# Opening stage of a two-layer hybrid trunk: own buffers for two streams of loads, and a written order on TensorE

## The chip, the core and the metric

The kernel runs on one core of a Trainium2 chip. The time is device microseconds of one execution, from several executions of the same program. The engines are named as the profile names them: PE (TensorE, products), PEld (its weight loads), DVE (VectorE), ACT (ScalarE), POOL (GpSimd) and SP (SyncE, whose queue issues the weight loads). Each engine works through its own instructions in the order in which they were built; semaphores tie the engines together.

## The reference, cut to what matters

Two layers run over 128 context tokens and 128 latent tokens that share all weights; the kernel takes both as one block of 256 columns. Ahead of each layer stand modulation vectors (shift, scale, gate) from a product of a conditioning vector with `w_mod`, and a normalisation that uses them:

```
m = jax.nn.silu(cond) @ w_mod + b_mod          # 2048 -> 6 x 2048, for c_ctx and for c
h = _rms_norm(x, norm1_g) * (1.0 + scale1) + shift1
p = h @ w_in                                   # gq gk gv gr glr aq ak av dqkv dz da db
```

Then follow gated linear attention, softmax attention and a gated DeltaNet on the parts of `p`, an output product, and a squared-ReLU MLP of four times the width. The opening stage of the kernel is the first layer's `m` (shift1 and scale1 only), `h`, and that part of `p` which needs only the first half of the 2048 inputs.

## The kernel before, in words

All products are made in three parts: a weight tile `raw` of 128 x 1024 numbers is loaded by SP (line 212, or 620 for the narrower first projection tiles), ACT copies it to `hi` in a shorter format, DVE makes `lo`, the rest, and PE multiplies `hi` with both halves of the activations and `lo` with the first. `hi` and `lo` have three buffers each.

`first_phase` (line 562) is the opening. It first makes `rstd`, the norm of each token. Then it walks over 16 chunks of 128 inputs, here called columns, n = 0 to 15:

- four modulation slices are loaded (line 593) and multiplied with the conditioning vectors (line 595, tile `mod0`, shown as mod); each slice makes 4 products, which the profile counts as 8 passes;
- ACT copies the result to `msb`; two small products turn it (line 601, `mod0t`); DVE adds the bias (`modc`), makes the scale `s` and the scaled chunk `ht`; ACT and DVE make both halves of the chunk `act` (`h_chunk`, line 492);
- for n < 8, two projection tiles are loaded, split and multiplied with the chunk (lines 619 to 633): 14 units of 3 products, into seven banks `fb`, `fbm`, `fbn`. At n = 7 the banks are copied out;
- for n >= 8, instead, a share of 45 half jobs is done (line 611): 3 tiles of `w_in` and 12 of `w_tok`, 3 steps each, which read only chunks 0 to 7 (tiles `g` and `gt`).

`mod0` and `mod0t` share one bank in `pmod`, so a column's slices can be multiplied only when DVE has read the turned result of the column before. All loads of the stage take buffers of one ring, `raw0`, with six buffers. A second ring of six, `wraw`, serves everything behind the opening.

The program is not issued in the order in which it is written: a scheduler with its own estimates orders each engine's instructions. Only products that bear the same token (`tok`, line 630: those of lines 631 to 633) keep their written order among each other. So the scheduler was free to set slices, turns and half jobs among the blocks, and to issue loads of the next stage early. The token of a product is given in `mm` (line 85).

Of the kernel before, what the change touches and what calls it, by code (L numbers as in the profile page):

```python
# [10 lines left out]
F32 = mybir.dt.float32  # L11
# [3 lines left out]
AF = mybir.ActivationFunctionType  # L15
ALU = mybir.AluOpType
AX = mybir.AxisListType
P = 128
# [23 lines left out]
def tile_hybrid_step(ctx: ExitStack, tc: tile.TileContext, A: dict, O: dict):  # L42
# [17 lines left out]
    ve, se = Timed(nc.vector, 1 / 960, 0.13), Timed(nc.scalar, 1 / 1400, 0.27)  # L60

    def pool(name, bufs=1, **kw):
        return tc.tile_pool(name=name, bufs=bufs, **kw)
# [3 lines left out]
    wraw = ctx.enter_context(pool("wraw", 6))  # L67
# [8 lines left out]
    pmod = ctx.enter_context(pool("pmod", 1, space=PS))  # L76
    dram = ctx.enter_context(pool("dram", 2, space=bass.MemoryType.DRAM))

    ntok = [0]

    def newtok():
        ntok[0] += 1
        return f"tok{ntok[0]}"

    def mm(out, lhsT, rhs, start=True, stop=True, tok=None, **kw):
        i = nc.tensor.matmul(out, lhsT=lhsT, rhs=rhs, start=start, stop=stop, **kw)  # L86
        n = math.prod(rhs.shape[1:])
        pe_t[0] += max(n / 2400 * (1 if rhs.dtype == F32R else 4), 0.027)
        if tok is not None:
            tc.stamp_issue_order_token(i.ins, tok)  # L90
        return i
# [39 lines left out]
    def open_act(tag, side="left"):  # L131
        st = ExitStack()
        pl = st.enter_context(pool(tag, side=side))
        return pl.tile([P, 16, 516], F32R, tag="act", name="act"), st

    act, actctx = open_act("acta")
# [19 lines left out]
    raw0 = rawctx.enter_context(pool("raw0", NRAW))  # L156
# [58 lines left out]
    def split_half(src, pl=None):  # L215
        raw = load_half(src, pl)
        hi = whi.tile([P, 1024], F32R, tag="hi", name="hi")
        lo = wlo.tile([P, 1024], F32R, tag="lo", name="lo")
        se.activation(hi, raw, AF.Copy)
        ve.tensor_tensor(lo, raw, hi.bitcast(F32), ALU.subtract)  # L220
        return hi, lo
# [66 lines left out]
    def gemm_pieces(src, halves, rhs_of, evac, pl=None):  # L288
        ps = pg.tile([P, 256], F32, tag="g", name="g")
        k0, k1 = 8 * halves[0], 8 * halves[-1] + 7  # L290
        for half in halves:
            hi, lo = split_half(src(half), pl)
            for q in range(2):
                for kk in range(4 * q, 4 * q + 4):
                    k = half * 8 + kk
                    a = rhs_of(k)
                    h = hi[:, kk * P : kk * P + P]
                    mm(ps, h, a[:, 0:256], start=(k == k0), stop=False)
                    mm(ps, h, a[:, 256:512], start=False, stop=False)
                yield  # L300
            for kk in range(8):
                k = half * 8 + kk
                mm(ps, lo[:, kk * P : kk * P + P], rhs_of(k)[:, 0:256], start=False, stop=(k == k1))
            if half == halves[-1]:
                evac(ps)
            yield
            if tick():
                yield
# [234 lines left out]
    def tsrc(w, n):  # L543
        return lambda half: w[n, half]

    def part_of(j):
        if j < 8:
            return lay["dqk"][:, j, :].rearrange("p (g t) -> p g t", g=2)
        if j < 12:
            return lay["vt"][:, :, (j - 8) * P : (j - 7) * P]  # L550
        t = lay["misc"] if j == 12 else lay["gqk"][:, j - 13, :]
        return t.rearrange("p (g t) -> p g t", g=2)

    def gq3(ps):
        return ps.rearrange("p (g t) -> p g t", g=2)

    def tok_dest(u, g):
        if u == 0:
            return lay["gv"][:, g, :]
        return lay["aq"][:, g, (u - 1) * 512 : u * 512] if u < 3 else lay["akv"][:, g, :]  # L560

    def first_phase(raw0):
        modc, s12, bm, ng = mods[0]
        X["np"] = raw0
        for n in range(16):
            accum_sq(n, n == 0)
        rate[0] = 0
        rstd = get_rstd()
        nb = len(FIRST)
        banks = [pg.tile([P, 512], F32, tag="g", name="fb") for _ in range(2)]  # L570
        banks += [pm.tile([P, 512], F32, tag="m", name="fbm") for _ in range(3)]
        banks += [pn.tile([P, 512], F32, tag="m", name="fbn") for _ in range(2)]
        tok = newtok()

        def half_jobs():
            for j in HALF_D:
                def evac(ps, j=j):
                    se.activation(part_of(j), gq3(ps), AF.Copy)

                yield from gemm_pieces(tsrc(A["w_in"][0], j), (0,), lambda k: act[:, k, 0:512], evac, raw0)  # L580
            for u in HALF_T:
                yield from gemm_tok(
                    lambda q, u=u: A["w_tok"][0][u, q], range(4),
                    lambda ps, g, u=u: se.activation(tok_dest(u, g), ps, AF.Copy), raw0,
                )

        jobs = half_jobs()
        njobs = 3 * len(HALF_D) + 12 * len(HALF_T)
        done = 0
        for n in range(16):  # L590
            ps = pmod.tile([P, 512], F32, tag="mod", name="mod0")
            for q in range(4):
                raw = load_half(A["w_mod0"][n, q], raw0)
                for kk in range(4):
                    mm(ps[32 * kk : 32 * kk + 32, 0:256], sc[:, 2 * (4 * q + kk) : 2 * (4 * q + kk) + 32], raw[:, kk * 256 : kk * 256 + 256],
                       start=(q == 0), stop=(q == 3), tile_position=(0, 32 * kk))
            msb = nrm.tile([P, 512], F32, tag="msb", name="msb")
            se.activation(msb[:, 0:256], ps[:, 0:256], AF.Copy)
            pt = pmod.tile([P, 512], F32, tag="mod", name="mod0t")
            for m in range(2):  # L600
                mm(pt[:, 2 * m : 2 * m + 2], msb[:, m * P : m * P + P], sel2)
            ve.tensor_tensor(
                modc[:, 0:2, n, :], pt[:, 0:4].rearrange("p (m c) -> p m c", m=2), bc(bm[:, 0:2, n], 2), ALU.add
            )
            ve.tensor_scalar(s12[:, 0, n, :], modc[:, 1, n, :], 1.0, ng[:, 0, n : n + 1], ALU.add, ALU.mult)
            t = X["np"].tile([P, 256], F32, tag="ht", name="ht", bufs=2)
            for g in range(2):
                s = slice(g * P, g * P + P)
                ve.scalar_tensor_tensor(t[:, s], X["x"][:, n, s], s12[:, 0, n, g : g + 1], rstd[:, s], ALU.mult, ALU.mult)
            h_chunk(n, t, modc[:, 0])  # L610
            if n >= 8:
                want = (n - 7) * njobs // 8
                while done < want:
                    next(jobs, None)
                    done += 1
                continue
            w = nb * 64
            for part in range(2):
                raw = raw0.tile([P, 1024], F32, tag="raw", name="raw")
                nc.sync.dma_start(raw[:, 0:w], A["w_in0"][n, part])  # L620
                hi = whi.tile([P, 1024], F32R, tag="hi", name="hi")
                lo = wlo.tile([P, 1024], F32R, tag="lo", name="lo")
                se.activation(hi[:, 0:w], raw[:, 0:w], AF.Copy)
                ve.tensor_tensor(lo[:, 0:w], raw[:, 0:w], hi[:, 0:w].bitcast(F32), ALU.subtract)
                for j in range(nb // 2):
                    u = part * (nb // 2) + j
                    o = banks[u // 2][:, (u % 2) * 256 : (u % 2) * 256 + 256]
                    h = hi[:, j * P : j * P + P]
                    l_ = lo[:, j * P : j * P + P]
                    kw = dict(tok=tok, skip_group_check=True)  # L630
                    mm(o, h, act[:, n, 0:256], start=(n == 0 and u % 2 == 0), stop=False, **kw)
                    mm(o, h, act[:, n, 256:512], start=False, stop=False, **kw)
                    mm(o, l_, act[:, n, 0:256], start=False, stop=(n == 7), **kw)
            if n == 7:
                for u, j in enumerate(FIRST):
                    src = gq3(banks[u // 2][:, (u % 2) * 256 : (u % 2) * 256 + 256])
                    if u % 4 < 2:
                        se.activation(part_of(j), src, AF.Copy)
                    else:
                        ve.tensor_copy(part_of(j), src)  # L640
        for _ in jobs:
            pass

# [9 lines left out]
    for l in range(L):  # L653
# [6 lines left out]
        else:  # L660
# [6 lines left out]
            act, actctx = nact, nactctx  # L667
# [157 lines left out]
        else:  # L825
            nlead = list(zip(FIRST, first))
            for j in FIRST[len(first) : 13]:
                for _ in range(2):
                    if nlead:
                        u, ps = nlead.pop(0)  # L830
# [841 lines left out]
```

## Time and profile before

| | |
|---|---|
| median of 3 runs | 2547.51 us (2547.04 to 2550.62) |
| the profiled execution | 2549.01 us, of which the span is 2547.2 us |
| mean granted clock | 0.993 |
| PE busy | 2482.5 us, 97% of the span |
| DVE, ACT busy | 1836.3 us (72%), 1246.1 us (49%) |

The span is what the profiler saw from the first instruction to the last; the time of the execution has some 2 us around it. Matmul ends in the profile are modelled, so that rows of PE can overlap a little: the distance between two starts tells more than a length. A number of passes (x8, x32) counts each product of 32-bit numbers twice. A wait in square brackets is the idle time of that engine just ahead of the row, with what ended it.

### The profile page before, as it was taken

Reading aid. Unit: us, or ns where it says so; the run is one execution under the profiler, and the core shown is the slowest. Engines: PE = TensorE matmul, PEld = TensorE weight load, DVE = VectorE, ACT = ScalarE, POOL = GpSimd, SP = SyncE. Lnnn points to the kernel's source line nnn. Section 1 sums busy time; section 2 is a strip of 40 time slices with the busy share of each in tenths; the row PEclk is TensorE's granted clock in tenths of the full one; section 3 lists DMA queues with packets and bytes.
Section 4 is the critical chain, followed back from the end, with each engine's and each line's share of the span. In section 5 each row is a group of like instructions: output and inputs, shape, how many; then the busy total and the mean of one; then the engine's idle time right before and its main releaser. Section 6 shows DMA issues by size and latency. Waiting matters only on the chain.

```text
span 2547.2 us, 47725 instructions
## 1 busy us (share of the span) xinstructions
PE 2482.5 (97%) x18796; PEld 2240.5 (88%) x18796; DVE 1836.3 (72%) x3478; ACT 1246.1 (49%) x2073; POOL 72.3 (3%) x108
## 2 busy tenths in 40 slices
PE   6999999999999999999999999999999999999999
PEld 4777677789899999999999888889999989999888
DVE  3456767658988898898897676786796564564665
ACT  3356244447554454444455763455675445445433
POOL 1000000000000100100100000000000000000000
PEclk9999999999999999999999999999999999999999
DMA  9975767785899999989996743446576666566564
GB/s 361 325 264 185 269 213 277 278 305 174 301 337 347 356 332 330 351 320 347 354 322 234 252 147 117 148 125 213 175 258 218 184 190 190 183 190 188 186 197 141
DMA packets 178993, 629.36 MB, mean 247 GB/s; under 512 B 21280, under 2 KB 28000, under 8 KB 177616
## 3 DMA queue, kind: packets, MB, share of 16 engines
q1 hardware_dynamic: 165600, 600.12, 68.4%
q0 software_dynamic: 10768, 22.94, 3.4%
q8 instruction: 148, 2.42, 0.4%
q10 hardware_dynamic: 2400, 3.24, 0.4%
q14 instruction: 77, 0.63, 0.1%
HBM read 613.62 MB, written 6.31 MB: 243 GB/s over the span
## 4 chain that ended last, share of the span: by engine, by line
PE 52%; ACT 1%; DVE 0%; DMA 0%; issue 0%; DVEq 0%; ACTq 0%
PE g L86 42%; PE gt L86 3%; PE gl L86 3%; PE mod L86 1%; PE ga L86 0%; ACT hi L56 0%; PE eb L86 0%; PE scb L86 0%; PE oatb L86 0%; PE xt L86 0%; PE yb L86 0%; PE ob L86 0%; PE bcb L86 0%; DMA x<-spill 0%; PE obg L86 0%; ACT L56 0%
## 5 line engine op out<-in xcount | busy, mean ns | idle before, releaser
L56 ACT ACTIVATE hi<-raw 128x1024 fp32r<-128x1024 f32 (+1 forms) x742 | 781.0, 1057 | 928.8 <-PE g L86 625.9
L56 DVE TENSOR_TENSOR lo<-raw,hi 128x1024 fp32r<-128x1024 f32 (+1 forms) x742 | 903.4, 1220 | 406.0 <-ACT hi L56 387.5
L86 PE MATMUL g<-act,hi 128*128 128x256 f32 (+1 forms) x7488 | 1053.5, 291 | 11.9 <-DVE x L56 3.8
L86 PEld LDWEIGHTS g<-act,hi 128*128 128x128 f32 x7488 | 955.6, 189 | 82.1 <-issue 22.3
L86 PE MATMUL g<-act,lo 128*128 128x256 f32 x4000 | 558.0, 282 | 2.8 <-DVE lo L56 2.8
L86 PEld LDWEIGHTS g<-act,lo 128*128 128x128 f32 x4000 | 512.8, 189 | 15.7 <-issue 4.8
L86 PE MATMUL g<-hid,hi 128*128 128x256 f32 (+1 forms) x1536 | 261.0, 319 | 0.0
L86 PEld LDWEIGHTS g<-hid,hi 128*128 128x128 f32 x1536 | 217.2, 189 | 22.1 <-ACT hi L56 4.2
L56 DVE SCALAR_TENSOR_TENSOR x<-g,modc,x 128x128 f32<-128x128 f32 x352 | 113.1, 348 | 149.5 <-PE g L86 144.3
L56 DVE CUSTOM_DVE_ANT_0 junk<-mraw,sb,bm 128x1024 bf16<-128x1024 f32 x160 | 205.0, 1281 | 2.4 <-DMA sb<-scd 0.9
L86 PE MATMUL mod<-raw,sc 128*32 128x512 f32 (+1 forms) x1216 | 144.1, 530 | 26.3 <-DMA raw<-w_mod 24.4
L56 DVE CUSTOM_DVE_ANT_0 junk<-mraw,sb,part 128x1024 bf16<-128x1024 f32 x128 | 164.1, 1282 | 5.2 <-DMA sb<-scd 4.7
L86 PE MATMUL gt<-hi,act 128*128 128x512 f32 x512 | 143.6, 412 | 3.9 <-ACT hi L56 3.9
L86 PE MATMUL g<-hid,lo 128*128 128x256 f32 x1024 | 141.6, 281 | 0.0
L86 PEld LDWEIGHTS g<-hid,lo 128*128 128x128 f32 x1024 | 134.5, 189 | 6.3 <-DVE x L56 0.8
L86 PEld LDWEIGHTS gt<-hi,act 128*128 128x128 f32 x512 | 94.8, 192 | 39.7 <-issue 11.1
L86 PEld LDWEIGHTS mod<-raw,sc 128*32 128x32 f32 x1216 | 29.4, 110 | 60.8 <-DMA raw<-w_mod 16.4
L86 PE MATMUL gt<-lo,act 128*128 128x512 f32 x256 | 75.1, 401 | 0.0
L86 PE MATMUL gl<-hid,hi 128*128 128x258 f32 x384 | 70.3, 286 | 2.1 <-ACT hi L56 2.1
L56 ACT ACTIVATE ffr<-g 128x256 f32<-128x256 f32 x116 | 42.9, 370 | 55.1 <-PE g L86 55.1
L56 ACT ACTIVATE xd<-g,modc 128x128 f32<-128x128 f32 x96 | 29.7, 360 | 68.1 <-PE g L86 68.1
L86 PEld LDWEIGHTS gl<-hid,hi 128*128 128x128 f32 x384 | 59.3, 189 | 2.6 <-ACT hi L56 2.5
(355 smaller groups left out, 1980.4 us busy)
## 6 DMA issues: line engine op xcount, KB each, us to landing
raw<-w_ff SPq DMA_DIRECT2D x512, 512.0 KB, 4.5
raw<-w_mod SPq DMA_DIRECT2D x240, 512.0 KB, 6.0
mraw<-w_modT SPq DMA_DIRECT2D x144, 512.0 KB, 6.2
raw<-w_in SPq DMA_DIRECT2D x86, 512.0 KB, 4.4
raw<-w_tok SPq DMA_DIRECT2D x64, 512.0 KB, 4.4
raw<-w_out SPq DMA_DIRECT2D x64, 512.0 KB, 4.3
sb<-scd POOLq DMA_DIRECT2D x9, 1024.0 KB, 9.5
raw<-w_in SPq DMA_DIRECT2D x16, 448.0 KB, 5.9
```

What stands on the lines that cost most here:

```text
L56: return f(out, *a, **kw)
L86: i = nc.tensor.matmul(out, lhsT=lhsT, rhs=rhs, start=start, stop=stop, **kw)
```

## The change

The opening's loads are put on two rings: the projection tiles of lines 619 and the half jobs go to `wraw`, the modulation slices keep `raw0`. The loop is written in another order, and while it runs every product of the stage bears one token, so PE keeps the written order: slices of column n + 1, then the block (or the half jobs) of column n, then the turn of column n + 1 and its chunk.

```diff
         i = nc.tensor.matmul(out, lhsT=lhsT, rhs=rhs, start=start, stop=stop, **kw)
...
+        if tok is None:
+            tok = cur[0]
         if tok is not None:
             tc.stamp_issue_order_token(i.ins, tok)
...
-                yield from gemm_pieces(tsrc(A["w_in"][0], j), (0,), lambda k: act[:, k, 0:512], evac, raw0)
+                yield from gemm_pieces(tsrc(A["w_in"][0], j), (0,), lambda k: act[:, k, 0:512], evac)
...
-                    lambda ps, g, u=u: se.activation(tok_dest(u, g), ps, AF.Copy), raw0,
+                    lambda ps, g, u=u: se.activation(tok_dest(u, g), ps, AF.Copy),
...
-        for n in range(16):
+
+        def columns(n):
             ps = pmod.tile([P, 512], F32, tag="mod", name="mod0")
...
+            return msb
+
+        def chunk(n, msb):
             pt = pmod.tile([P, 512], F32, tag="mod", name="mod0t")
...
+
+        def outer(n):
             w = nb * 64
             for part in range(2):
-                raw = raw0.tile([P, 1024], F32, tag="raw", name="raw")
+                raw = wraw.tile([P, 1024], F32, tag="raw", name="raw")
...
+        cur[0] = newtok()
+        chunk(0, columns(0))
+        for n in range(16):
+            msb = columns(n + 1) if n < 15 else None
+            if n < 8:
+                outer(n)
+            else:
+                want = (n - 7) * njobs // 8
+                while done < want:
+                    next(jobs, None)
+                    done += 1
+            if n < 15:
+                chunk(n + 1, msb)
+        cur[0] = None
```

How the order of the instructions moves is shown at three places. First PE, around the end of a block in the middle of the opening, before (x4 here is one slice, the numbers behind mod name the column):

```order
L86 MATMUL fbn<-act,hi 128x256 x2
L86 MATMUL fbn<-act,lo 128x256
L86 MATMUL mod_718<-raw,sc 32x256 x4
L86 MATMUL mod0t<-c_sel_97,msb 128x2 x2
L86 MATMUL mod_811<-raw,sc 32x256 x12
L86 MATMUL fb<-act,hi 128x256 x2
```

and the same place after:

```order
L86 MATMUL fbn<-act,hi 128x256 x2
L86 MATMUL fbn<-act,lo 128x256
L86 MATMUL mod0t<-c_sel_97,msb 128x2 x2
L86 MATMUL mod_757<-raw,sc 32x256 x16
L86 MATMUL fb<-act,hi 128x256 x2
```

Before, one slice of the column stood behind the block and three ahead of it; after, all four slices of the next column stand ahead of the block, and the turn follows the block directly.

Second DVE, one middle column before, from modc to the next modc:

```order
L56 TENSOR_TENSOR modc<-mod0t,bm 128x2x2
L56 TENSOR_SCALAR s_147<-modc,ng 128x2
L56 SCALAR_TENSOR_TENSOR ht<-x,s_147,rstd 128x128 x2
L56 SCALAR_TENSOR_TENSOR act<-ht,modc,act 128x128 x2
L56 TENSOR_TENSOR lo<-raw,hi 128x896 x2
L56 TENSOR_TENSOR modc<-mod0t,bm 128x2x2
```

and after:

```order
L56 TENSOR_TENSOR modc<-mod0t,bm 128x2x2
L56 TENSOR_SCALAR s_147<-modc,ng 128x2
L56 SCALAR_TENSOR_TENSOR ht<-x,s_147,rstd 128x128 x2
L56 TENSOR_TENSOR lo<-raw,hi 128x896
L56 SCALAR_TENSOR_TENSOR act<-ht,modc,act 128x128 x2
L56 TENSOR_TENSOR lo<-raw,hi 128x896
L56 TENSOR_TENSOR modc<-mod0t,bm 128x2x2
```

One of the two lo of a column now stands between ht and act.

Third SP's loads at the start, before (w_in 128x1024 are tiles of the stage behind the opening, w_in 128x896 the first projection tiles, w_mod the slices):

```order
L129 DMA x<-xT 128x1024 x4
L212 DMA raw<-w_mod 128x1024 x4
L620 DMA raw<-w_in 128x896 x2
L212 DMA raw<-w_in 128x1024 x6
L212 DMA raw<-w_mod 128x1024 x4
```

and after, where the lines have moved by two and by one:

```order
L131 DMA x<-xT 128x1024 x4
L214 DMA raw<-w_mod 128x1024 x6
L621 DMA raw<-w_in 128x896 x6
L214 DMA raw<-w_mod 128x1024 x6
L621 DMA raw<-w_in 128x896 x3
```

The six early tiles of the next stage are gone from the start; six projection tiles stand where two stood, behind six slices where four stood.

## Rows read from the trace of the kernel before

**Rows 1.** Busy time by stretch: stretch, length, five engines, granted clock, DMA share, GB/s.

```profile
0.00:171.20 171.20, 138.59 (x1135) 102.88 (x1135) 75.75 (x173) 64.38 (x119) 9.37 (x21) 0.97 0.89 328
171.20:2547.20 2376.00, 2343.88 (x17662) 2137.59 (x17662) 1760.54 (x3306) 1181.68 (x1955) 62.92 (x87) 0.99 0.71 241
```

**Rows 2.** Instructions in time, PE, a middle column: start, length, operation, [wait before].

```profile
65.22 0.64 PE L86 MATMUL mod<-raw,sc 128*32 128x256 f32 x8
66.37 0.61 PE L86 MATMUL mod0t<-c_sel,msb 128*128 128x2 f32 x4 [0.50 <-ACT msb L56]
67.23 1.50 PE L86 MATMUL mod<-raw,sc 128*32 128x256 f32 x24 [0.25 <-DVE modc L56]
68.66 0.72 PE L86 MATMUL fb<-act,hi 128*128 128x256 f32 x2
...
74.10 0.64 PE L86 MATMUL mod<-raw,sc 128*32 128x256 f32 x8
```

**Rows 3.** Instructions in time, PE, columns 0 and 1.

```profile
19.56 1.08 PE L86 MATMUL mod<-raw,sc 128*32 128x256 f32 x8 [1.65 <-DMA raw<-w_mod]
...
25.54 0.97 PE L86 MATMUL fb<-act,hi 128*128 128x256 f32 x2 [2.32 <-ACT act L56]
...
30.36 0.48 PE L86 MATMUL fbm<-act,hi 128*128 128x256 f32 x2
...
32.93 1.50 PE L86 MATMUL mod<-raw,sc 128*32 128x256 f32 x24
...
34.72 0.64 PE L86 MATMUL mod<-raw,sc 128*32 128x256 f32 x8 [0.28 <-DMA raw<-w_mod]
...
47.72 1.07 PE L86 MATMUL mod<-raw,sc 128*32 128x256 f32 x16
```

**Rows 4.** Instructions in time, PE, from column 7's end to the first product behind.

```profile
101.46 0.64 PE L86 MATMUL mod<-raw,sc 128*32 128x256 f32 x8
102.03 2.15 PE L86 MATMUL g<-act,hi 128*128 128x256 f32 x16
...
104.96 0.40 PE L86 MATMUL g<-act,hi 128*128 128x256 f32 x2
...
127.60 2.13 PE L86 MATMUL gt<-hi,act 128*128 128x512 f32 x8
129.56 0.50 PE L86 MATMUL mod0t<-c_sel,msb 128*128 128x2 f32 x4
...
151.13 0.64 PE L86 MATMUL mod<-raw,sc 128*32 128x256 f32 x8 [0.74 <-DMA raw<-w_mod]
...
153.50 3.62 PE L86 MATMUL gt<-hi,act 128*128 128x512 f32 x8 [0.56 <-ACT hi L56]
...
171.19 2.17 PE L86 MATMUL g<-act,hi 128*128 128x256 f32 x16 [0.79 <-ACT aq L56]
```

**Rows 5.** Busy time by stretch, four stretches of 4 us.

```profile
28.00:32.00 4.00, 4.00 (x27) 4.00 (x26) 0.00 (x0) 0.00 (x0) 0.00 (x0) 1.00 1.03 410
40.00:44.00 4.00, 3.89 (x25) 2.98 (x22) 0.93 (x4) 0.78 (x3) 0.00 (x0) 0.50 1.01 381
132.00:136.00 4.00, 4.00 (x36) 2.59 (x28) 0.79 (x3) 0.98 (x4) 0.00 (x0) 1.00 1.02 410
144.00:148.00 4.00, 4.00 (x32) 2.88 (x24) 1.90 (x5) 0.75 (x2) 0.00 (x0) 1.00 0.72 211
```

**Rows 6.** Instructions in time, SP's queue, loads of the start.

```profile
11.16 9.38 SPq L212 DMA_DIRECT2D raw<-w_in  x6
...
20.78 4.00 SPq L212 DMA_DIRECT2D raw<-w_mod  x4
```

**Rows 7.** Instructions in time, DVE, the column of rows 2.

```profile
62.98 2.24 DVE L56 TENSOR_TENSOR lo<-raw,hi 128x896 fp32r<-128x896 f32 x2 [3.09 <-ACT hi L56]
...
67.01 0.16 DVE L56 TENSOR_TENSOR modc<-mod0t,bm 128x4 f32<-128x4 f32 x1 [1.79 <-PE mod0t L86]
...
68.30 0.64 DVE L56 SCALAR_TENSOR_TENSOR act<-ht,modc,act 128x128 fp32r<-128x128 f32 x2 [0.21 <-ACT act L56]
```

## What is expected of the change

> **What bounds the kernel now.** I read the busy times by stretch first: up to 171.2 us TensorE (PE) is busy 138.6 us at a granted clock of 0.97, while the DMA engines stand at 0.89 and 328 GB/s; the other 2376 us hold PE at 99% with DMA at 0.71 [rows 1]. So what PE does not need it can save only in the opening, and everything behind 171.2 us is a row of products that starts earlier if the opening ends earlier. The opening makes 16 columns: 4 modulation slices each (mod), a turn of the result (mod0t), a normalised chunk (act), and for columns 0 to 7 a block of 42 products (fb); behind column 7 come half jobs (g, gt). PE's own row of instructions shows where it loses time.
>
> One middle column, fast clock: the last slice's mod (8 passes) begins at 65.22, mod0t waits 0.50 for the copy msb, mod of the next column waits 0.25 for modc on VectorE (DVE) and starts 0.86 behind mod0t, the first pair of fb takes 0.72, and the next column's mod begins at 74.10 [rows 2]. A column is thus 8.88 us. From the end of the block of column 1 (47.72) to that of column 7 (101.46) six columns take 53.74 us, 8.96 each [rows 3, 4]; DMA rates move between 211 and 410 GB/s in the opening [rows 5], so the transfers pause for buffers and are not the steady limit.
>
> **The change part by part.** No product, transfer or copy is added or dropped; orders, rings and with them waits change. Three stretches.
>
> *Start, up to the end of the block of column 1.* Before, six loads for the stage behind (3.15 MB at 524 KB each) are issued at 11.16 to 20.54 us, ahead of column 1's slices at 20.78 [rows 6]; its last slice is there at 34.72 [rows 3]. After, the six are gone from there, but four more 459 KB projection loads stand ahead of that slice: 3.15 less 1.84 MB is 1.31 MB, at the 410 GB/s of that stretch [rows 5] 3.2 us, so it lands at 31.5. The fixed order now puts column 1's slices ahead of the block of column 0, which was ready at 25.54 [rows 3]. PE has been idle for much of that time, so the slice's 8 passes take 1.08 us as at 19.56 [rows 3] and the block starts at 32.6, 7.1 us later than before. Before, the block ran at the slow level (1.2 GHz) until 30.36 (7 of its 14 units in 4.82 us) and took 7.4 us in all [rows 3]. A block at the fast level takes 5.05 (68.66 to 74.10, 5.44, less a wait that I put at 0.39, of which 0.32 shows: the first pair takes 0.72 where an undisturbed pair of that shape takes 0.40, at 104.96 [rows 2, 4]). I take 6.8, nearer the cold one since PE idles ahead of it: end 39.4. Now mod0t of column 1 follows at once, since msb was copied under the block. With the column worked out next, 8.64 us, the block of column 1 ends at 48.0 against 47.72: 0.3 us lost. Bounds: 5.05 instead of 6.8 makes 1.5 gained; 7.4 and a slice 1.5 us later (the steps between two slices' arrivals are about that) 2.4 lost.
>
> *Columns 2 to 7.* Per column PE has mod0t to mod 0.86, 32 passes of mod 1.91 (24 take the 1.43 from 67.23 to 68.66 [rows 2]) and the block 5.05: 7.82 us. The 0.50 for msb is gone, as is the time in which the last 8 passes stood alone ahead of mod0t. What is late next is act. On DVE modc begins 0.64 behind mod0t's start and act ends at 68.94, 2.57 behind [rows 2, 7]. In the new order one lo stands between ht and act; it takes 1.12 (2.24 for two) and covers the 0.21 that act waited for ScalarE (ACT) anyway, so act is done 2.57 + 1.12 - 0.21 = 3.48 behind mod0t. The second product of the block reads it. Before, the block with its wait taken out counts from 74.10 - 5.05 = 69.05, 0.11 behind act's end; now it counts from 3.59 behind mod0t, not from the 2.77 at which PE is through with mod: 0.8 us of wait, with the rest of the block and the next mod0t queued behind it on PE and nothing else to fill it. Column: 3.59 + 5.05 = 8.64, against 8.96; times six, 1.9 us gained. Bounds: if act were not late 7.82, 6.8 us; if lo also waits for its own tile and another 0.3 per column goes, nothing. I take 1.9, since lo's buffer comes free when the block before ends, ahead of modc.
>
> *From the end of the block of column 7 to the first product behind the opening.* Before 101.46 to 171.19: 69.7 us [rows 4]. After, on PE: 7 mod of 1.91 = 13.4; 7 times 0.86 and a last 0.5 for mod0t = 6.5; three half jobs of 2.93 (102.03 to 104.96) and twelve of 2.85 (1.96 for the two hi groups, 127.60 to 129.56, and about 0.9 for lo) = 43.0 [rows 4]; together 62.9. To it come 0.8 for the last copy (aq, as before), 0.3 for modc of column 8 behind the copies of the banks, 0.9 for modc of column 15 behind a lo whose buffer comes free only just ahead of it, and 0.1 of rounding: 65.0. What goes is what stood between: waits for slices, such as 0.74 at 151.13, for msb and for hi (0.56), and the slow group at 153.50 behind them, 3.62 where 2.13 is usual [rows 4]. The projection loads have buffers of their own, so a slice no longer waits for a lo. Gain 4.7; bounds: 6.8 with none of the last four, and 0.7 if 0.5 per column is added for waits that stay.
>
> *Behind the opening* the rows of PE are the same but for a few swaps. The six tiles loaded early are now three; a tile feeds 24 products, 2.9 us, and brings 524 KB, 1.3 us at 410 GB/s, under a PE that is full: nothing, with 1.3 us if the first comes late. The swaps later I put at 0, with 2 us either way.
>
> Sum: -0.3 + 1.9 + 4.7 = 6.3 us less. The profiled execution took 2549.0 us, its span 2547.2, so 2542.7 by it; it is 1.5 over the median of the runs, 2547.5, and by that the forecast is 2541.2, put as 2541.
>
> **The rivals.**
> *Transfers set the pace in the later columns.* For: 0.89 DMA over the opening. A later column loads 4 slices and 15/8 tiles, 3.08 MB; at the mean of 328 GB/s [rows 1] that is 9.4 us, over the 8.1 that PE needs, and at 410 it is 7.5, under it. Against: 410 was reached at 132 to 136 us, and 211 soon behind, at 144 to 148 [rows 5], so the engines bring more when loads are there to be brought. At 360, midway, 8.55: 0.4 lost on each of 8, the gain is 3 or so, 2544; at 328 nothing is left, 2548.
> The Trainium skill (DMA: Bandwidth & Descriptors, Specifications) gives about 358 GB/s as one core's limit from HBM. By that figure this rival would be right at 2544, an estimate; the trace had 410 GB/s over 4 us, twice [rows 5], so the measurement speaks against it as a cap.
>
> *Act is not late, and the clock stays up from the start.* 6.8 in the middle, 1.5 at the start, 5 behind: 13 us, 2534. For: lo may run before ht is ready. Against: DVE works in the order given.
>
> *PE stalls at the slices (slower).* Now all four slices of a column stand ahead of a block that is ready. A column's third and fourth slice take the buffers of the first two of the column before, so they are issued one column ahead. With a full queue of loads a slice took 10 us from issue to landing (column 1's last, issued by 24.78, used at 34.72 [rows 3, 6]); at one column's 8.64 plus 1.8 this just decides. If landing takes 12 us, 1.6 us are lost in each of 14 columns, and each such wait can bring the granted clock of 0.50, the level of 1.2 GHz, that 40 to 44 us shows [rows 5]: 22 less 6.3, about 16 slower, 2563. Against: once the rings are full only what a column set free is queued.
>
> *The edit does nothing there*: start and act eat the gain, 2547.
>
> **How the numbers follow.** A measurement of this kernel can tell 0.2%, 5.1 us, from no change. Forecast (3 to 11 us faster) 0.66, of which 0.48 is over 5.1; transfers 0.12 and no effect 0.06, both within; no wait at all 0.10, faster; slower 0.06. Faster 0.58, same 0.36, slower 0.06. The range, 2533 to 2548, takes in the bounds added up and leaves out the slower case.
>
> **What would show it.** In the changed profile: column 1's last slice near 31.5 us and the first fb near 32.6; mod0t 8.6 us apart in the middle columns; no wait of mod0t for msb; the second product of a block held about 0.8 us by DVE's act; the first g behind the opening near 165 us instead of 171.2. It is wrong if mod waits for slices in most columns, or if the granted clock falls in the middle of the opening.

## The result and the profile after

The changed kernel takes 2533.48 us (median of 4 runs, 2531.67 to 2535.32) against 2547.66 us (4 runs, 2547.04 to 2550.62) beside it: a ratio of 0.9945, 95% interval 0.9932 to 0.9959, 14.2 us faster. The forecast was 2541 us: the direction holds, the time lies within the range of 2533 to 2548, but by half a microsecond only, and the gain is more than twice the 6.3 us of the sum. The profiled execution took 2533.5 us, its span 2531.7 us (before 2547.2), its mean granted clock 0.995 (before 0.993). PE is busy 2469.7 us of it, DVE 1837.6 us.

By the starts on PE's row the 15.5 us of span divide as follows. The second pair of columns is another execution of each kernel, from the experiments below.

| stretch | before | after | gain | forecast | second pair, gain |
|---|---|---|---|---|---|
| start to the end of the block of column 1 | 47.72 | 47.08 | 0.6 | -0.3 | 47.58, 48.81: -1.2 |
| columns 2 to 7 | 53.74 | 48.94 | 4.8 | 1.9 | 53.53, 49.01: 4.5 |
| from there to the first g behind the opening | 69.73 | 64.93 | 4.8 | 4.7 | 70.58, 65.08: 5.5 |
| from that g to the end of the span | 2376.0 | 2370.7 | 5.3 | 0 | 2374.7, 2365.2: 9.5 |

The stretches of the changed kernel, with the columns of [rows 1]:

```profile
0.00:160.95 160.95, 131.12 (x1135) 100.91 (x1135) 75.12 (x173) 65.11 (x119) 9.38 (x21) 0.98 0.93 351
160.95:2531.70 2370.75, 2338.59 (x17662) 2135.46 (x17662) 1762.51 (x3306) 1181.53 (x1955) 62.93 (x87) 1.00 0.71 242
```

The opening holds the same 1135 products as up to 171.2 us in [rows 1] and ends 10.2 us earlier; DMA goes from 328 to 351 GB/s. Behind it the count of products is equal too, so the 5.3 us there are not work that was moved.

PE at the start, to be held against [rows 3]:

```profile
30.92 1.08 PE L86 MATMUL mod<-raw,sc 128*32 128x256 f32 x8 [6.16 <-DMA raw<-w_mod]
32.20 1.08 PE L86 MATMUL mod<-raw,sc 128*32 128x256 f32 x8 [0.20 <-DMA raw<-w_mod]
33.21 0.80 PE L86 MATMUL fb<-act,hi 128*128 128x256 f32 x2
...
38.89 0.50 PE L86 MATMUL mod0t<-c_sel,msb 128*128 128x2 f32 x4
39.65 1.93 PE L86 MATMUL mod<-raw,sc 128*32 128x256 f32 x32 [0.26 <-DVE modc L56]
47.08 0.51 PE L86 MATMUL mod0t<-c_sel,msb 128*128 128x2 f32 x4
```

Column 1's last slice is used at 32.20, the block of column 0 starts at 33.21, and mod0t follows it at 38.89 without a wait.

PE in a middle column, which answers to [rows 2]:

```profile
55.23 0.50 PE L86 MATMUL mod0t<-c_sel,msb 128*128 128x2 f32 x4
55.99 1.94 PE L86 MATMUL mod<-raw,sc 128*32 128x256 f32 x32 [0.26 <-DVE modc L56]
57.85 0.38 PE L86 MATMUL fb<-act,hi 128*128 128x256 f32 x1
58.43 0.39 PE L86 MATMUL fb<-act,hi 128*128 128x256 f32 x1 [0.19 <-DVE act L56]
```

and DVE in the same column, which answers to [rows 7]:

```profile
55.77 0.16 DVE L56 TENSOR_TENSOR modc<-mod0t,bm 128x4 f32<-128x4 f32 x1 [0.87 <-PE mod0t L86]
55.97 0.23 DVE L56 TENSOR_SCALAR s<-modc,ng 128x2 f32<-128x2 f32 x1
56.23 0.61 DVE L56 SCALAR_TENSOR_TENSOR ht<-x,s,rstd 128x128 f32<-128x128 f32 x2
56.76 1.08 DVE L56 TENSOR_TENSOR lo<-raw,hi 128x896 fp32r<-128x896 f32 x1
57.77 0.61 DVE L56 SCALAR_TENSOR_TENSOR act<-ht,modc,act 128x128 fp32r<-128x128 f32 x2
```

The one lo stands between ht and act, and the second product of the block is held until act ends at 58.38: the wait that was named, but of 0.19 us and not 0.8. The starts of lo and act also lie some 0.07 us ahead of the end of the row before them (56.76 against 56.23 + 0.61, 57.77 against 56.76 + 1.08).

The waits of PE in the whole opening, first of after, then the three largest of before (us in total, times, longest):

```profile
PE mod L86 <- DMA raw<-w_mod: 8.7, 4, 6.2
PE mod L86 <- DVE modc L56: 4.9, 14, 1.3
PE fb L86 <- DVE act L56: 1.5, 7, 0.3
PE mod0t L86 <- ACT msb L56: 0.5, 1, 0.5
```

```profile
PE mod L86 <- DMA raw<-w_mod: 20.3, 10, 12.8
PE mod0t L86 <- ACT msb L56: 4.9, 9, 0.6
PE gt L86 <- ACT hi L56: 2.5, 4, 1.2
```

After column 1 no slice is waited for at all. Last, PE from the end of block 7, for [rows 4]:

```profile
96.02 0.50 PE L86 MATMUL mod0t<-c_sel,msb 128*128 128x2 f32 x4
...
144.70 0.50 PE L86 MATMUL mod0t<-c_sel,msb 128*128 128x2 f32 x4
146.46 1.91 PE L86 MATMUL mod<-raw,sc 128*32 128x256 f32 x29 [1.26 <-DVE modc L56]
...
160.95 2.18 PE L86 MATMUL g<-act,hi 128*128 128x256 f32 x16 [0.76 <-ACT aq L56]
```

### The profile page after: what moved, and what is told of

The parts are those of the page before. It is cut to its first block, busy times and chain, and to the rows that moved or that the text cites. A ratio compares the mean times of both kernels' runs of the same rounds, so it can differ in the third digit from the quotient of the medians.

```text
span 2531.7 us, 47749 instructions
## 1 busy us (share of the span) xinstructions
PE 2469.7 (98%) x18796; PEld 2236.4 (88%) x18796; DVE 1837.6 (73%) x3478; ACT 1246.6 (49%) x2073; POOL 72.3 (3%) x108
## 4 chain that ended last, share of the span: by engine, by line
PE 53%; ACT 1%; DVE 0%; DMA 0%; issue 0%; DVEq 0%; ACTq 0%
PE g L86 42%; PE gt L86 3%; PE gl L86 3%; PE mod L86 1%; PE ga L86 0%; ACT hi L56 0%; PE eb L86 0%; PE oatb L86 0%; PE scb L86 0%; PE ob L86 0%; PE xt L86 0%; PE yb L86 0%; PE bcb L86 0%; DMA x<-spill 0%; PE obg L86 0%; ACT L56 0%
## 5 line engine op out<-in xcount | busy, mean ns | idle before, releaser
L86 PEld LDWEIGHTS g<-act,lo 128*128 128x128 f32 x4000 | 513.4, 189 | 12.8 <-issue 4.9
```

## The experiments

Two theories of the size were put up. One: the gain is the opening's, rings and order together, and act behind a lo is what still holds the columns. The other: a part of the gain is the granted clock behind the opening, which the opening does not set. The clock's part is read in two ways: from stretches of 2 us with a granted clock under 1, and over many runs as (1 - granted clock) x span, called the clock loss below. The clock is given to a thousandth, so that one run's loss is known to 1.3 us, a mean over runs better. The loss is read from the granted clock alone; the last section shows where PE was slow though it read 1.00.

**Rings alone.** The kernel before with the projection tiles and half jobs on `wraw`; the order is the scheduler's.

```diff
-                raw = raw0.tile([P, 1024], F32, tag="raw", name="raw")
+                raw = wraw.tile([P, 1024], F32, tag="raw", name="raw")
```

Expected: 

> The rings alone: projection tiles and half jobs on the standing ring, order left to the scheduler. Theory A (the written order gives the middle columns their gain, the rings give the start and the late columns theirs): the end of the block of column 1 comes near 44 to 46 us, the six columns to the end of column 7 stay at 8.7 to 9.0 us each, the late part takes 66 to 67, so the first product behind the opening starts near 164 us; about 2538 to 2541 us in all. Theory B (what counts is that loads no longer share buffers, the order hardly matters): columns near 8.2, opening over near 161, 2533 to 2535 us. Behind the opening both expect some 2371 us, give or take 3.4 for half-clock stretches that come and go.

Measured: 2538.24 us (12 runs), ratio 0.9965 (0.9952 to 0.9977). The first small product behind the opening (tile pgb, of the next stage; the scheduler mixes the g products of both stages here, so that the first g is no mark) comes 6.0 us earlier than before (177.35 against 183.35; after 173.11). In its first columns PE still waits for msb and act,

```profile
43.22 0.61 PE L86 MATMUL mod0t<-c_sel,msb 128*128 128x2 f32 x4 [0.56 <-ACT msb L56]
45.46 0.97 PE L86 MATMUL fb<-act,hi 128*128 128x256 f32 x2 [1.63 <-ACT act L56]
...
72.32 0.50 PE L86 MATMUL mod0t<-c_sel,msb 128*128 128x2 f32 x4
...
80.49 0.50 PE L86 MATMUL mod0t<-c_sel,msb 128*128 128x2 f32 x4
```

but columns 5 to 8 stand 7.9 to 8.3 us apart with no order written down. The scheduler hides msb in these columns only: 7 waits for it stay in the opening (3.8 us in all; before 9 and 4.9). The time is what theory A gave, the columns are those of theory B. The turn of column 8 stands at 96.87, between the 96.02 and 97.82 of the two executions of the changed kernel; what is missing is lost later, around the last two columns, where PE waits 1.1 us for msb, 1.9 for act and 1.4 for slices (159 to 168 us). So the rings bring more than half of the gain, and the gain up to column 7 does not need the written order.

**Order alone.** The changed kernel with every load of the opening back on `raw0`.

```diff
-                raw = wraw.tile([P, 1024], F32, tag="raw", name="raw")
+                raw = raw0.tile([P, 1024], F32, tag="raw", name="raw")
```

Expected: 

> The written order alone: all loads of the opening stay on one ring of six buffers, and the scheduler brings the six early tiles of the next stage again. Theory A: column 1's last slice comes 2 us or more later than in the changed kernel and the tiles of column 0 behind it, end of column 1 near 50 us; columns 8.2 where loads are in time, up to 9 where they are not; late part 67 to 70; opening over at 168 to 172 us, so about 2541 to 2547 us. Theory C (the order is all of it, rings do nothing): opening over near 161 us, 2533 to 2535 us.

Measured: 2555.66 us (12 runs), ratio 1.0029 (1.0018 to 1.004): 7 us slower than before, where both theories had it faster, and the first g behind the opening at 177.05 instead of 171.19. PE, the block of column 0 and that of column 1:

```profile
34.86 0.80 PE L86 MATMUL fb<-act,hi 128*128 128x256 f32 x2 [1.53 <-ACT hi L56]
35.99 0.58 PE L86 MATMUL fb<-act,lo 128*128 128x256 f32 x1 [0.33 <-DVE lo L56]
...
45.81 0.50 PE L86 MATMUL fb<-act,hi 128*128 128x256 f32 x2 [0.28 <-ACT hi L56]
46.94 0.38 PE L86 MATMUL fb<-act,lo 128*128 128x256 f32 x1 [0.63 <-DVE lo L56]
```

On SP's queue the six early tiles of the next stage stand again from 10.72 to 20.34 us, and the tiles of the block of column 0 come behind them and two of column 1's slices, at 23.31; after, they are issued from 10.56 on. The blocks wait for hi and lo (2.8 us in all behind 33 us) and more for act (7.6, after 1.5); the slices themselves cost 1.3. So this fixed order does not pay on one ring.

**Act ahead of lo.** The changed kernel, with a token on DVE so that act of columns 1 to 6 is made before the next lo.

```diff
+            if g == 1 and 0 < k < 7:
+                tc.stamp_issue_order_token(i_.ins, f"dv{k}")
...
+                if part == 0 and n > 1:
+                    tc.stamp_issue_order_token(i_.ins, f"dv{n - 1}")
```

Expected: 

> The changed kernel with DVE held to finish a column's act before it makes the next lo (columns 1 to 6). If act behind lo is what a middle column waits for, as predicted, the block counts from PE's own 2.77 us behind mod0t in place of 3.2: six columns of 7.7 to 7.8 us where the changed kernel has 8.16, the opening over 2.2 to 2.7 us earlier, near 158.5 us; about 2531 us. Rival: transfers then set the pace (3.01 MB in 7.75 us is 388 GB/s); PE waits for slices and the columns stay at 8.1 or over.

Measured: 2528.35 us (6 runs), ratio 0.9924 (0.9906 to 0.9942). DVE in a middle column, and mod0t of PE in two:

```profile
54.64 0.16 DVE L56 TENSOR_TENSOR modc<-mod0t,bm 128x4 f32<-128x4 f32 x1 [0.87 <-PE mod0t L86]
...
55.93 0.64 DVE L56 SCALAR_TENSOR_TENSOR act<-ht,modc,act 128x128 fp32r<-128x128 f32 x2 [0.21 <-ACT act L56]
56.49 1.08 DVE L56 TENSOR_TENSOR lo<-raw,hi 128x896 fp32r<-128x896 f32 x1
```

```profile
93.54 0.50 PE L86 MATMUL mod0t<-c_sel,msb 128*128 128x2 f32 x4
101.21 0.50 PE L86 MATMUL mod0t<-c_sel,msb 128*128 128x2 f32 x4
```

Act ends 2.47 us behind mod0t instead of 3.15, the block waits for nothing, the columns take 7.65 to 7.8 us and the first g comes at 158.53. So a late act was what held the columns at 8.16, and by 0.4 us.

**The block of column 0 ahead of column 1's slices.** The changed kernel, in the order that the forecast priced at 7 us.

```diff
+            if n == 0:
+                outer(0)
...
-            if n < 8:
+            if n == 0:
+                pass
+            elif n < 8:
```

Expected: 

> The changed kernel with the block of column 0 ahead of the slices of column 1 again. If the 7 us for which that block stands behind the slices cost time, as predicted in the start's sum, it starts near 25 us and runs while the slices land, mod0t of column 1 comes near 35 in place of 38.9 and the opening is over 3 to 4 us earlier, near 157.5 us; about 2530 us. Rival: the loads set the start, what is won is waited for again at the slices of column 2, and under 1 us is left.

Measured: 2536.39 us (8 runs), ratio 0.995 (0.9933 to 0.9967).

```profile
34.59 0.61 PE L86 MATMUL mod0t<-c_sel,msb 128*128 128x2 f32 x4 [0.50 <-ACT msb L56]
...
41.28 1.08 PE L86 MATMUL mod<-raw,sc 128*32 128x256 f32 x8 [4.76 <-DMA raw<-w_mod]
...
49.87 0.50 PE L86 MATMUL mod0t<-c_sel,msb 128*128 128x2 f32 x4
```

The first turn comes 4.3 us earlier (34.59 against 38.89) and the second 2.8 us later (49.87 against 47.08, and 1.1 later than the 48.81 of the other execution): column 2's slices are waited for in its place, as the rival has it. The block behind that wait also begins at a granted clock of 0.50, up to 46 us. Loads, more than the order on PE, set the start.

**The kernel before once more.**

Expected: 

> The kernel before, unchanged, run and profiled once more: what belongs to the program must come again, what belongs to one execution need not. Theory C (the half-clock stretches behind the opening follow PE's own pauses, and those come from the order of the instructions): the wait of the second qkb for E is again 1.8 to 2.1 us and a half-clock stretch of 1.7 us or more lost follows it; the stretch at 1430 comes again as well. Rival D (they are phase or chance): the wait comes again, but the stretches stand elsewhere, and the time is within the 2540 to 2556 us seen so far with no fixed place for them. Median 2546 to 2550 by both.

Measured: 2546.08 us (12 runs), against 2547.96 us of the runs beside it, which are the same program: 0.9985 (0.9974 to 0.9997). A ratio within 0.15% of 1 therefore says nothing here. In the gated DeltaNet behind the opening the products qkb wait for E, an exponential that ACT makes. The second group of qkb and the stretch around it, in the first profile of before and in this one:

```profile
237.73 1.19 PE L86 MATMUL qkb<-dqk 128*128 128x128 f32 x8 [1.96 <-ACT E L56]
```

```profile
236.00:252.00 16.00, 14.27 (x58) 7.16 (x58) 11.81 (x18) 5.87 (x7) 0.54 (x1) 0.79 0.49 165
```

```profile
239.47 1.16 PE L86 MATMUL qkb<-dqk 128*128 128x128 f32 x8 [2.39 <-ACT E L56]
```

```profile
236.00:252.00 16.00, 13.61 (x71) 7.49 (x70) 11.93 (x18) 7.59 (x9) 0.54 (x1) 1.00 0.48 175
```

With a longer wait (2.39 against 1.96) the granted clock stays at 1.00. Theory C, that the length of the pause decides, fails here; rival D holds for this place. The one at 1430 comes again (3.4 us lost at 1426 to 1434), as C has it.

**The changed kernel once more.**

Expected: 

> The changed kernel, unchanged, run and profiled once more, beside the kernel before on the same chip. Theory C: qkb waits about 1.64 us for E and no half-clock stretch stands in 225 to 240; the longer stretch near 630 and the one near 1850 come again; ratio 0.9935 to 0.996. Rival D: a half-clock stretch stands behind qkb here though the program is the same; the opening's 10 us are certain (first small product behind the opening again within 0.5 us of 173.1), and the other 4 come and go; ratio 0.995 to 0.997.

Measured: 2534.01 us (6 runs), ratio 0.9938 (0.9919 to 0.9957). The first small product comes at 175.07, not within 0.5 of 173.11: the block of column 0 ran slower (see the last section). Only 4.3 us are lost to the clock in this profile (12.8 in the first), and no half-clock stretch stands behind qkb, though it waits 2.03 us here and not 1.64. The one near 630, which C wanted again, did not come, nor did that at 28 to 36; the one near 1850 did. So C and D each miss a part.

**Loads of the start in written order.** On the kernel with act ahead of lo: column 1's slices ahead of all projection tiles, then by turns.

```diff
+                raw = load_half(A["w_mod0"][n, q], raw0, "ld" if n < 3 else None)
...
+                if n < 2:
+                    tc.stamp_issue_order_token(i_.ins, "ld")
```

Expected: 

> The kernel of the lo order (act of columns 1 to 6 ahead of the next lo) with the first loads kept in written order on SP: column 1's four slices ahead of all projection tiles, then two tiles, column 2's slices, two tiles. Theory A (the start is set by which loads stand ahead): column 1's last slice lands near 27, its block 0 starts near 28, mod0t of column 1 stands at 34 instead of 38.7, column 2's slices are there in time (mod waits under 1 us), the opening ends 4 us earlier, first g behind it at 154 to 155; 2524 us. Rival B (the transfers already run at 395 to 406 GB/s from 20 to 120 us in that kernel, so they set the pace and the start's gain is waited for at slices of later columns): mod0t of column 1 at 34 too, but mod waits for slices in columns 2 to 9, 3 us or more together, and the first g behind the opening stays within 1.5 us of 158.5; 2527 to 2530 us.

Measured: 2530.9 us (6 runs), ratio 0.9925 (0.9905 to 0.9944).

```profile
28.81 0.50 PE L86 MATMUL fb<-act,hi 128*128 128x256 f32 x2 [1.54 <-ACT hi L56]
29.93 0.39 PE L86 MATMUL fb<-act,lo 128*128 128x256 f32 x1 [0.63 <-DVE lo L56]
...
36.28 0.50 PE L86 MATMUL mod0t<-c_sel,msb 128*128 128x2 f32 x4
...
40.35 0.39 PE L86 MATMUL fb<-act,hi 128*128 128x256 f32 x1 [0.71 <-DVE act L56]
45.34 0.50 PE L86 MATMUL mod0t<-c_sel,msb 128*128 128x2 f32 x4
```

Mod0t of column 1 comes at 36.28 against 38.68, not at 34: the tiles, loaded later, are split later, and the block waits for hi and lo. The first g stands at 157.12 against 158.53. No later column waits for a slice, so B's mechanism is wrong as well, though its number is the nearer one. The 1.4 us do not show in the time.

**Both exponentials ahead of the logarithm.** On the kernel with act ahead of lo: far behind the opening, ACT makes both E of the first layer before it loads the table of the logarithm.

```diff
+            if l == 0:
+                nE.append(g)
+                tc.stamp_issue_order_token(i_.ins, "eln")
...
+                while l == 0 and len(nE) < 2:
+                    yield
```

Expected: 

> The kernel of the lo order, with one order changed far behind the opening: ScalarE makes both E of the first layer ahead of its first logarithm, so that no table load stands between them; the same products, in another order around it. Theory C (the pause of PE brings the half clock): PE's wait of 2.39 us for E at 226 goes, no granted clock under 0.95 stands in 222 to 240, and by 260 us the products are 4 to 5 us earlier, 2.4 of it the wait and the rest the clock; 2524 us. Rival D (the half clock comes by chance or by phase): the wait goes, a half-clock stretch stands there or close by all the same, gain 2 or less. Rival E (the stretch is put off: another pause of PE later in the run is answered by a longer fall): the clock stays up here, and the stretches behind grow by as much; total unchanged, 2528 us.

Measured: 2531.79 us (6 runs), ratio 0.9933 (0.9914 to 0.9951). The same stretch in the kernel that it starts from, and here:

```profile
222.00:240.00 18.00, 15.61 (x65) 8.24 (x65) 11.99 (x18) 8.06 (x10) 0.54 (x1) 0.72 0.33 112
```

```profile
222.00:240.00 18.00, 18.00 (x90) 10.49 (x88) 15.16 (x35) 10.82 (x14) 0.54 (x1) 1.00 0.52 181
```

The wait and the half clock are gone and 90 products stand where 65 did, yet the time is not shorter. The stretch at 626 to 636 lost 3.4 us here, 1.7 in the other; but the edit also reorders many products behind it, and the span without the clock loss is no shorter either (2522.1 against 2518.6). So the time of theory C did not come, and neither D nor E is shown. Where the gain was given back is not settled.

**The changed kernel, put off.** Five tiny loads, each behind the one before, ahead of the first load; the loads of x and of column 0 behind them are held in the written order.

```diff
+        if tag == "i":
+            for _ in range(5):
+                i_ = nc.sync.dma_start(X["x"][:, 0, 0:32], src[:, 0, 0:32])
+                tc.stamp_issue_order_token(i_.ins, "ld")
...
```

Expected: 

> The changed kernel with five tiny loads of a corner of x, each behind the one before, ahead of its first load: no product added, and the products in the changed kernel's order, but all of it later by the time of these five (about 2 us each, 10 us), so that the stages behind the opening start about when they did in the kernel before the change. Theory Q (the clock part of the gain comes from PE's own pauses, which are those of the changed kernel): the full-clock time lost, (1 - granted clock) x span as a mean over the runs, stays at the changed kernel's 8 us, and the time is 2534 plus the shift, 2544. Rival R (it comes from when the stages start): it goes to the 17 to 18 us of the kernel before, and the time is 2534 plus the shift plus 9, 2553. Between 11 and 15 us lost neither is shown.

Measured: 2543.93 us (11 runs), ratio 0.9982 (0.9974 to 0.9991). The first g stands at 168.47, 7.5 us later than after and only 2.7 earlier than before; the opening keeps a granted clock of 1.00 from 25 us on. The clock loss is 10.2 us (95%: plus or minus 2.2), within error of the changed kernel's and well under the 17 to 18 of before. That speaks against rival R: the clock part does not come from the time at which the stages start. But with the shift of 7.5 us theory Q gives 2541 us and R some 2550, so the time is 2.4 over Q. Behind the opening this profile takes 2375.3 us, as before does, so the gain there is not in it; its order differs there in a few places, and what cost it is not shown.

**The kernel with act ahead of lo, once more.**

Expected: 

> The fastest of the variants (act of columns 1 to 6 ahead of the next lo), unchanged, run and profiled once more beside the kernel before. If its 2528 us was the order of DVE (6.3 us less than the changed kernel, of which the columns show 2.4): first g behind the opening again within 1.5 us of 158.5, ratio 0.9910 to 0.9935. If part of it was a lucky clock: the same opening, but 2530 to 2533 us and a ratio of 0.993 to 0.9945, with the full-clock time lost at 8 us or more instead of 6.7.

Measured: 2530.59 us (5 runs), ratio 0.9934 (0.992 to 0.9947), first g at 158.85, clock loss 12.1 us: the second of the two cases. The order of DVE gives the 2 to 4 us that the opening shows; the rest of the 2528 was clock. It beats both kernels, the changed one by some 3 us, and no other variant is clearly faster.

All runs together (mean and its 95% error, us; before counts the runs beside the experiments and the repeat):

| kernel | runs | span | clock loss | span less loss |
|---|---|---|---|---|
| before | 69 | 2546.4 | 17.5, 0.8 | 2528.9, 0.4 |
| after | 10 | 2531.6 | 9.6, 2.2 | 2522.0, 1.8 |
| rings alone | 12 | 2536.3 | 14.0, 1.8 | 2522.4, 0.6 |
| order alone | 12 | 2553.9 | 15.7, 2.4 | 2538.2, 2.7 |
| act ahead of lo | 11 | 2527.8 | 9.2, 3.1 | 2518.6, 1.9 |
| block 0 first | 8 | 2533.9 | 12.0, 3.7 | 2521.9, 1.2 |
| loads ordered | 6 | 2528.1 | 10.5, 4.9 | 2517.5, 2.4 |
| E ahead of the logarithm | 6 | 2530.1 | 8.0, 1.1 | 2522.1, 2.2 |
| after, put off | 11 | 2542.3 | 10.2, 2.2 | 2532.2, 1.6 |

Among the 69 runs of before the span rises by 0.92 us for each us of clock loss, so the loss is worth about its own length in time. The rings alone and the changed kernel differ by 4.7 us of span, but without the clock loss they are level (2522.4 and 2522.0): on this reckoning the rings bring the whole gain that is not clock, and what the written order adds to them shows as a smaller clock loss (9.6 against 14.0), for which no cause is shown.

## Why the prediction was right in sign and short in size

*The start* was forecast at 0.3 lost and came at 0.6 gained and, in the second pair, 1.2 lost: within the bounds. The slice came at 32.20 (forecast 31.5), the block at 33.21 (32.6), and the block took 5.68 in one execution and 6.99 in the other (6.8). The forecast put the block of before at the level of 1.2 GHz until 30.36; the granted clock reads 1.00 there [rows 5], and only the pace of the products bears the level out (last section). The experiment with the block of column 0 first shows that the 7 us by which it starts later cost next to nothing, since the loads would have been waited for one column later.

*Columns 2 to 7* is the mis-sized term: 4.8 and 4.5 instead of 1.9, 8.16 a column and not 8.64. The mechanism was right, though act was late by 0.2 us and not by 0.8, and the experiment with act ahead of lo shows it. Of the 0.53 us in the column shown (8.11 from mod0t to mod0t), 0.39 are the chain on DVE: its lengths were added one behind the other, with one lo at 1.12, while the rows overlap, so that lo sets act back by 1.01 and modc starts 0.54 and not 0.64 behind mod0t; act ends 3.15 behind it, not 3.48, and PE goes on 0.05 behind that, not 0.11. The other 0.14 are the block, 4.91 from there and not 5.05, a length that was taken from a difference of two estimates of a wait.

*From block 7 on* 64.93 and 65.08 against 65.0: the named terms hold one by one. Aq is 0.76 (forecast 0.8), modc of column 15 costs 1.26 where others cost 0.26 (forecast 0.9 more), and the waits for slices, msb and hi are gone. One wait of 0.71 us, of gt for ACT's copy gv, was not in the sum.

*Behind the opening* 0 plus or minus 2 was forecast and 5.3 and 9.5 came. This is the step that failed. It counted products and transfers and took the clock of before for granted, although the page of before showed a clock of 0.993, a loss of 18 us. Over the runs 14.8 us of span divide into 6.9 (plus or minus 1.8) without and 7.9 (2.3) with the clock: the part that was worked out, 6.3, is about what the 6.9 are, and the clock more than doubled it. That the two agree so well is partly luck, since the term of columns 2 to 7 was short by 2.7 us. In the opening 5.1 and 3.4 us were lost in the two profiles of before, 3.4 and none after; the none is the reading of the granted clock, not PE's pace (last section), and why the loss fell is not shown. Why it also fell behind the opening, by 3.1 and 5.9 us in the profiles, stays open: the kernel that was put off speaks against the time at which the stages start; the repeats show that the pause ahead of qkb does not decide it by its length; and of those 5.3 and 9.5 us some 2 to 3.5 are not clock by this reckoning.

*The range* was said to take in the bounds added up. Added up, the bounds of the four terms (15.1 and 2 us better, 1.7 and 2 us worse) give 2530 to 2551 us, wider than 2533 to 2548; the measured time lay just inside the narrower one.

*The rivals.* That act is not late and the clock up, 2534 us, had the number nearest to the measured one for a reason that did not occur: act is late in seven columns, and the start of the first profile ran at 0.50. That transfers set the pace is refuted: no slice is waited for after 32.20 us, and the columns go at 8.16 us. The kernel with act ahead of lo moves 390 to 406 GB/s in each stretch of 20 us from 20 to 120 us. The Trainium skill (DMA: Bandwidth & Descriptors, Specifications) puts one core's limit from HBM at about 358 GB/s; the measurement is over it for 100 us, so as a cap on this core it does not hold here. That PE stalls behind a fixed order did not occur after, but it is what the order does with one ring, 7 us slower; there PE waits more for act, hi and lo (10.4 us) than for slices (1.3).

## What to carry to other kernels

Give loads with different consumers rings of their own before fixing an order: the rings alone gave 10 us of span, the order alone lost 7, both gave 15, and of what both gave beyond the rings nothing clear of the error is left once the clock loss is taken out. When a chain of short instructions on one engine sets a wait, take the starts of the rows and not their lengths. Where the page shows a granted clock under 1, work out what is lost to it and let the range of a forecast hold a change of that loss; it was as large as the change itself.

## What the runs showed of the hardware

One program, unchanged, lost 4.3 and 12.8 us to the clock in two executions (after), 13.7 and 17.6 (before), with pauses of PE at nearly the same places. One pause of 2 us (1.96) is followed by the 1.2 GHz level in one execution, and a longer one (2.39) is not in the next. The Trainium skill (TensorE: Matmul & The Clock Gate, What's actually happening) says that the gate's watch runs free and is not set anew when a kernel starts. The two pauses agree with it, and no run here shows more of the cause.

The granted clock does not tell the whole pace of PE. In the second execution of the changed kernel the block of column 0 ran slow for longer than in the first (until 38.15 and 34.66 us), at a granted clock of 1.00. PE, two pairs of products of it, and the stretch in which the first pair stands; below them the same stretch of the first execution, and a pair of the kernel before, from a stretch whose granted clock is 0.50 [rows 5]:

```profile
37.01 0.63 PE L86 MATMUL fbm<-act,hi 128*128 128x256 f32 x2
...
38.15 0.40 PE L86 MATMUL fbm<-act,hi 128*128 128x256 f32 x2
```

```profile
36.00:38.00 2.00, 2.00 (x11) 2.00 (x11) 0.00 (x0) 0.00 (x0) 0.00 (x0) 1.00 1.03 399
```

```profile
36.00:38.00 2.00, 2.00 (x20) 2.00 (x20) 0.42 (x1) 0.95 (x1) 0.00 (x0) 1.00 1.02 393
```

```profile
42.02 0.63 PE L86 MATMUL fb<-act,hi 128*128 128x256 f32 x2
```

A pair of the same shape takes 0.63 and 0.40 us, and 11 products stand in 2 us where the first execution has 20 at the same granted clock of 1.00. The 0.63 is the pace of the 1.2 GHz level, as the pair of the kernel before has it. That kernel's block of column 0 also went at 0.63 us a pair until 30.36 us, at 1.00 [rows 5]. PE had been idle for 6.09 us ahead of column 1's third slice. So the clock loss above is short of what the start of an execution loses, and a loss of none in the opening, as read there for this execution and for the kernel that was put off, does not mean that PE ran at full pace.
